# Attention with whole probabilities and one masked triangle of value differences; steps around two stage boundaries and the last norm rewritten

## The chip, the cores and the metric

The kernel runs on one core of one Trainium2 chip. The metric is the device time of one execution in microseconds (us); the time of a kernel is the median of its runs. The engines are named as in the profile: PE is TensorE (matrix products), DVE is VectorE, ACT is ScalarE, POOL is GpSimd, and SP is SyncE, which here only issues DMA transfers.

## The reference

One layer over 1024 tokens of width 2048, all in float32. What is computed:

```
h = x @ w_in + b_in                      # 2048 -> 4352 columns: q, k, v, g_attn, u_pool, g_pool
a = attention(q, k, v) * silu(g_attn)    # 16 heads of 64, 2 key/value heads, window 128, sinks, relative bias
b = pool(u_pool) * silu(g_pool)          # trailing means over 2, 4, 8, 16 tokens, minus the token, a linear map
mix = concat(a, b) @ w_out
ple = sigmoid(x @ w_gate_ple) * (p @ w_ple)
out = layer_norm(2 ** 0.25 * x + mix + ple)

# attention, for each block of 128 queries q against the block before (old) and its own block (cur):
e = exp(scores - m);  probs = e / (sum(e) + exp(sink - m))
out = probs @ [v_old; v_cur]
```

In a block, query `qq` sees the keys of the block before at positions above `qq`, and those of its own block at positions up to `qq`. So the two halves of a row of probabilities fill complementary triangles of one 128 by 128 matrix.

## The kernel before, in words

**Products.** Every large product (`x @ w_in`, `x @ w_gate_ple`, `mix @ w_out`) is done by a Strassen-Winograd scheme: seven products `p1` to `p7` in place of eight, on operand sums named `b11`, `b21`, `b22`, `t1` to `t4` (the activations' side) and on sums of weight quarters. A float32 operand is split into a high part and a rest in the fp32r format (`wh` and `wl` for weights, `b11h` and `b11l` and so on for activations), and one product is three fp32r matmuls, `wh*xh`, `wh*xl`, `wl*xh` (`mm3`, L180 to L185), over four slices of 128: twelve matmuls. The casts to the high part run on ACT (`copy`, L802 to L808, shown as L805), the rests on DVE (`lo`, L131, shown as L126 like all of DVE's two-input operations). Weight splits are made four products ahead (`take`, L245; the pool `w` has four buffers).

**Jobs and groups.** A `Job` is a pair of 128-row output blocks, and a group is one job or two side by side (`run_group`, L439). After each product the program's own clock `tick()` (L162) moves one step. `after(n, fn)` puts a step n ticks on; `later(n, fn)` does the same and makes the step's instructions stand behind the latest marked instruction of each engine (L167). A scheduler orders each engine's queue under these constraints; each queue then runs in order. Results are copied from the PSUM banks `qa`, `qb`, `sc` into tiles named `part` or `d`: by ACT for the first contribution (L421), by DVE for the second (`gather`, L416). When a job is through, `finished` (L429) adds the other half from DRAM by an accumulating DMA on POOL's queue (L434, `part<-h`), and `job.wait` ticks later `job.done` uses the tile.

**Stages** (L1123 to L1139, run from L1235 on): s1 and s2 make q, k, v and the first halves of the rest; while s2 runs, the 16 calls of `heads` (L562) do attention between the products, nine ticks apart (L1267). s3 makes second halves, with gates, pooling and the embedding gate in `done`. Its last four jobs are the attention gates: `gate_attn` (L683) applies SiLU on ACT (L685), multiplies on DVE and stores to `cc`. During its last two groups `set_by_twos` (L392) loads the operands of the next stage in pairs of tiles `two` and splits them (ACT casts, DVE rests). s4 and s5 are the output product for the two halves of its inner dimension, s5 over the first 768 tokens; s6 does the last 256 tokens with plain products (`run_plain`, L497). The last two jobs of s5 add straight onto loaded tiles (`filled`, `add_to`).

**Attention.** `heads` works on two heads for 512 queries. Per block of 128 queries: `score` (L585, scores on PE, bias and row maximum on DVE), `softmax` (L606, exponentials on ACT; L617 adds the old half onto the current half on POOL, which is lawful because the triangles don't overlap), `share` (L619, division by the sum). Per pair of blocks `trans` (L625) transposes on PE, casts the high part on ACT (L632), takes the rest on DVE (L633), and on POOL cuts each of the two into two triangles (L639): four selections of 128 by 512. `value` (L643) then multiplies the four triangles of a block with the values of the block before and of its own: four matmuls. Work tiles `s` come from the pool `slots` (16 buffers).

**Norm.** The squares are summed over blocks in s5 and s6; `norm_scale` (L1010) forms one over the standard deviation per token as a column (POOL's power, L1019), makes it a diagonal matrix (ACT L1024, or for the last 256 tokens DVE L1027) and multiplies by a matrix of ones, so that each partition holds the row of scales (L1007 and L1033). `norm_out` and `norm_out_two` apply it and store the output.

## Time and profile before

| what | value |
|---|---|
| time, median of 3 runs (lowest to highest) | 1461.7 us (1460.07 to 1462.81) |
| the profiled execution: its own time, and its span | 1460.25 us, 1458.5 us |
| VectorE, ScalarE and GpSimd busy, share of the span | 1120.4 us (77%), 788.9 us (54%), 292.6 us (20%) |
| mean granted clock of TensorE | 0.996 |
| DMA | 307.67 MB, mean 211 GB/s |

A span runs from the first to the last instruction; 1.75 us of the profiled execution's time lie around it. A row of the time line gives the start, the length, the engine, the line, the operation and its tiles, and in brackets how long the engine stood idle before it and what ended that. Matmuls overlap, so that the distance from one start to the next tells more than a length. A row of stretches gives busy microseconds of PE, of weight loads, DVE, ACT and POOL with counts, then the granted clock, the busy share of the DMA engines and GB/s.

### The profile page before, as it was taken

The page shows a single profiled execution, that of the slowest core. Times are in us where ns is not written, and L with a number is a line of the kernel's source. Part 1 is how long each engine was busy: PE and PEld are TensorE (multiplying, and loading weights), DVE is VectorE, ACT ScalarE, POOL GpSimd, SP SyncE. Part 2 cuts the span into 40 slices and gives each one's busy share as a digit, 9 for nine tenths or more (in the row PEclk, how much of TensorE's full clock was granted, in tenths as well). Part 3 has the DMA queues.
Part 4 walks back from the last instruction along what each step waited for, and adds up shares of the span by engine and source line. Part 5 has one row for each costly group of instructions (what it writes and reads, how often), then busy time and mean ns, then how long its engine had stood idle before and what let it go on. Part 6 is the DMA issues. An engine that isn't in the chain of part 4 may idle for free.

```text
span 1458.5 us, 20547 instructions
## 1 busy us (share of the span) xinstructions
PE 1435.3 (98%) x6930; PEld 1216.8 (83%) x6930; DVE 1120.4 (77%) x2031; ACT 788.9 (54%) x1560; POOL 292.6 (20%) x412
## 2 busy tenths in 40 slices
PE   9999999999999999999999999999998999999996
PEld 7888888888888888888888888888887888899996
DVE  6859578888787887888777876866777566977786
ACT  6546376565665666566655444333456333554475
POOL 1000203333233332223011111211001111111233
PEclk9999999999999999999999999999999999999998
DMA  9463885554456555557787779998698778595465
GB/s 356 181 242 117 235 222 180 172 176 152 138 181 209 182 170 176 183 194 234 200 248 221 200 216 317 318 290 247 191 347 255 190 189 232 133 268 114 120 240 207
DMA packets 112297, 307.67 MB, mean 211 GB/s; under 512 B 12800, under 2 KB 18304, under 8 KB 112192
## 3 DMA queue, kind: packets, MB, share of 16 engines
q1 hardware_dynamic: 87552, 225.88, 45.1%
q0 software_dynamic: 21312, 73.15, 21.2%
q10 hardware_dynamic: 3328, 7.34, 1.5%
q8 instruction: 54, 0.88, 0.3%
q14 instruction: 51, 0.42, 0.1%
HBM read 207.75 MB, written 98.57 MB: 210 GB/s over the span
## 4 chain that ended last, share of the span: by engine, by line
PE 64%; issue 22%; DVE 5%; POOL 4%; ACT 3%; DMA 2%; POOLq 0%; SPq 0%; ACTq 0%; DVEq 0%
PE qa L183 11%; PE qa L185 11%; PE qa L184 11%; PE qb L183 8%; PE qb L184 8%; PE qb L185 8%; POOL part L434 2%; PE sc L594 1%; PE pv L652 1%; DVE s L126 1%; DVE wl L126 1%; PE tr L630 1%; DMA part<-h 1%; DVE part L126 1%; PE sc L183 1%
## 5 line engine op out<-in xcount | busy, mean ns | idle before, releaser
L805 ACT CAST wh<-raw 128x512 fp32r<-128x512 f32 x428 | 264.0, 619 | 395.8 <-PE qa L184 143.5
L126 DVE TENSOR_TENSOR wl<-raw,wh 128x512 fp32r<-128x512 f32 x428 | 300.1, 705 | 108.6 <-ACT wh L805 105.5
L421 ACT COPY part<-qa 128x512 f32<-128x512 f32 (+1 forms) x180 | 103.9, 577 | 78.6 <-PE qa L185 76.2
L639 POOL TENSOR_SCALAR_AFFINE_SELECT s<-s 128x512 fp32r<-128x512 f32 x128 | 102.5, 813 | 132.2 <-ACT s L632 97.0
L126 DVE TENSOR_TENSOR part<-part,qb 128x512 f32<-128x512 f32 (+1 forms) x120 | 81.1, 676 | 46.4 <-PE qb L185 39.3
L183 PE MATMUL qa<-b11h,wh 128*128 128x512 f32 (+2 forms) x292 | 109.4, 375 | 0.8 <-ACT wh L805 0.8
L183 PE MATMUL qb<-b21h,wh 128*128 128x512 f32 (+2 forms) x292 | 109.2, 374 | 0.0
L185 PE MATMUL qa<-b11h,wl 128*128 128x512 f32 (+2 forms) x292 | 108.8, 373 | 0.0
L184 PE MATMUL qa<-b11l,wh 128*128 128x512 f32 (+2 forms) x292 | 108.7, 372 | 0.0
L185 PE MATMUL qb<-b21h,wl 128*128 128x512 f32 (+2 forms) x292 | 108.6, 372 | 0.0
L184 PE MATMUL qb<-b21l,wh 128*128 128x512 f32 (+2 forms) x292 | 108.6, 372 | 0.0
L183 PE MATMUL qb<-t1h,wh 128*128 128x512 f32 (+1 forms) x260 | 101.3, 390 | 3.5 <-ACT wh L805 2.0
L183 PE MATMUL qa<-t3h,wh 128*128 128x512 f32 (+1 forms) x260 | 100.6, 387 | 2.0 <-ACT part L421 2.0
L183 PE MATMUL qa<-t2h,wh 128*128 128x512 f32 (+1 forms) x260 | 100.8, 388 | 1.1 <-ACT part L421 0.5
L185 PE MATMUL qa<-t2h,wl 128*128 128x512 f32 (+1 forms) x260 | 99.9, 384 | 0.7 <-DVE wl L126 0.7
L183 PE MATMUL qb<-b22h,wh 128*128 128x512 f32 (+1 forms) x260 | 100.4, 386 | 0.0
L184 PE MATMUL qb<-t1l,wh 128*128 128x512 f32 (+1 forms) x260 | 100.3, 386 | 0.0
L185 PE MATMUL qb<-t1h,wl 128*128 128x512 f32 (+1 forms) x260 | 100.2, 386 | 0.0
L183 PE MATMUL qa<-t4h,wh 128*128 128x512 f32 (+1 forms) x260 | 100.1, 385 | 0.0
L184 PE MATMUL qa<-t3l,wh 128*128 128x512 f32 (+1 forms) x260 | 99.7, 384 | 0.0
L185 PE MATMUL qb<-b22h,wl 128*128 128x512 f32 (+1 forms) x260 | 99.7, 383 | 0.0
L184 PE MATMUL qb<-b22l,wh 128*128 128x512 f32 (+1 forms) x260 | 99.7, 383 | 0.0
(330 smaller groups left out, 3567.1 us busy)
## 6 DMA issues: line engine op xcount, KB each, us to landing
raw<-in_win SPq DMA_DIRECT2D x65, 512.0 KB, 4.1
h<-part SPq DMA_DIRECT2D x34, 512.0 KB, 2.9
part<-h POOLq DMA_DIRECT2D x34, 512.0 KB, 6.5
cw<-in_wout SPq DMA_DIRECT2D x64, 256.0 KB, 3.2
raw<-in_wgate SPq DMA_DIRECT2D x32, 512.0 KB, 4.8
raw<-wc SPq DMA_DIRECT2D x32, 512.0 KB, 4.5
s<-in_x SPq DMA_DIRECT2D x44, 256.0 KB, 6.3
wc<-cw SPq DMA_DIRECT2D x32, 256.0 KB, 2.4
```

The lines of the kernel that those rows point to most:

```text
L126: return (eng or self.nc.vector).tensor_tensor(out=out, in0=a, in1=b, op=op)
L183: mm(ps, wh, xh, start=start, stop=False, skip_group_check=True)
L184: mm(ps, wh, xl, start=False, stop=False, skip_group_check=True)
L185: return mm(ps, wl, xh, start=False, stop=stop, skip_group_check=True)
L421: self.mark("ACT", self.nc.scalar.copy(out=dst, in_=ps))
L434: self.nc.gpsimd.dma_start(out=t, in_=job.first(job.b[i]), accum_op=ALU.add)
L594: nc.tensor.matmul(ps[:, e, z:], q, kk[:, keys], start=i == 0, stop=i == 1)
L630: nc.tensor.transpose(ps[:, o : o + P], sc[bq + i][:, e, P:], self.ident)
L639: nc.gpsimd.affine_select(out=o4, in_=a4, pattern=[[0, 4], [sign, P]], compare_op=ALU.is_ge, fill=0.0, base=0 if side else -1, channel_mul ...
L652: nc.tensor.matmul(ps[:, bq % 2], self.vv[b // 4][:, b % 4], pt[bq // 2, s, i][:, o : o + 256], start=(s, i) == ms[0], stop=(s, i) == ms[-1])
L805: ins = self.nc.scalar.copy(out=out, in_=a)
```

## The change

**Attention.** `trans` keeps the transposed probabilities whole: per block it casts the high part and the rest (two casts and two rests of 128 by 256 where there was one of each of 128 by 512), and POOL cuts one triangle, the old one, of both parts at once: one selection of 128 by 512 per block, none for the first block of the sequence. `value` multiplies the whole with the values of the own block, and the old triangle with the differences (values of the block before minus own values), so that the sum is the same. `v_build` makes these differences (`vd`, new tiles `d0`, `d1`) by copies on ACT and subtractions on DVE. Their room is taken from the work tiles: 15 of 512 columns while attention runs, then 16 of 528 again in s3.

**End of s3.** Three more `part` buffers (8 where there were 5), 4 buffers for operand pairs (6 before), 8 work tiles (10 before); pairs are loaded two units ahead of their split instead of three, the first at ticks 5 and 7 (0, 3 and 6 before). The last two jobs wait 5 and 6 ticks (3 and 3 before) for `done`, their second blocks one tick more.

**s5 and s6.** Weight casts of the `filled` and plain jobs are marked, so that steps put off by `later` stand behind them on ACT. The plain operand of s6 (`last_operand`) is split at ticks 6, 8, 10 and 12 of the last group of s5 by `later`, instead of in code behind it. `norm_scale` makes no diagonal matrix: PE takes the column itself, read 128 times, as the stationary matrix, and the identity as the moving one, 128 columns at a time.

**Start.** One weight half of the embedding is loaded and split ahead of the second half of `p`, and the second and third early product change places.

The diff, cut to its core (the line numbers of the order's rows for the changed kernel are its own):

```
     def __init__(self, w, b0, b1, half, first, done, tokens=2 * T, plain=False, ahead=None):
-        self.ahead, self.filled, self.mean, self.wait = ahead, False, False, 4
+        self.ahead, self.filled, self.mean, self.apart, self.wait = ahead, False, False, False, 4
...
-        self.unit_latest = [self.copy(hi, src).ins, L.lo(lo, src, hi).ins]
+        cast = self.copy(hi, src)
+        if job.filled or job.plain:
+            self.mark("ACT", cast)
+        self.unit_latest = [cast.ins, L.lo(lo, src, hi).ins]
...
             self.split_unit(u, r.pop(u))
-            fetch(i + 3)
+            fetch(i + 2)
...
-            fetch(0)
-            self.after(3, lambda: fetch(1))
-            self.after(6, lambda: fetch(2))
+            self.after(5, lambda: fetch(0))
+            self.after(7, lambda: fetch(1))
...
-        self.later(job.wait, lambda: job.done(job.b[i], t))
+        self.later(job.wait + (i if job.apart else 0), lambda: job.done(job.b[i], t))
...
-            nc.scalar.copy(out=v[:, :, 0:64], in_=ps[:, :, g])
-            self.lo(v[:, :, 64:128], ps[:, :, g], v[:, :, 0:64])
+            d = self.vd[h] = self.tile(self.kv, [P, 3 + h, P], f"d{h}", F32R)
+            at = slice(1 - h, 4)
+            s = self.slot()
+            v32, d32 = (s[:, i * 256 : i * 256 + 256].rearrange("p (b d) -> p b d", b=4) for i in range(2))
+            nc.scalar.copy(out=v32, in_=ps[:, :, g])
+            nc.scalar.copy(out=v[:, :, 0:64], in_=v32)
+            self.lo(v[:, :, 64:128], v32, v[:, :, 0:64])
+            if h:
+                self.tt(d32[:, 0], self.vv[0][:, 3, 0:64].bitcast(F32), v32[:, 0], ALU.subtract)
+                self.tt(d32[:, 0], d32[:, 0], self.vv[0][:, 3, 64:128].bitcast(F32), ALU.add)
+            self.tt(d32[:, 1:4], v32[:, 0:3], v32[:, 1:4], ALU.subtract)
+            nc.scalar.copy(out=d[:, :, 0:64], in_=d32[:, at])
+            self.lo(d[:, :, 64:128], d32[:, at], d[:, :, 0:64])
...
-            hi, lo = self.slot(), self.slot()
-            nc.scalar.copy(out=hi.bitcast(F32R)[:, :T], in_=ps)
-            self.tt(lo.bitcast(F32R)[:, :T], ps, hi[:, :T], ALU.subtract)
-            for i, a in enumerate((hi, lo)):
-                for side, o in enumerate((self.slot(F32R), a)):
...
+            for i in range(2):
+                t = ps[:, 2 * i * P : 2 * i * P + 2 * P].rearrange("p (e q) -> p e q", e=2)
+                both = pt[bq + i] = self.slot(F32R)[:, :T].rearrange("p (s e q) -> p s e q", s=2, e=2)
+                nc.scalar.copy(out=both[:, 0], in_=t)
+                self.lo(both[:, 1], t, both[:, 0])
+                if not k0(bq + i):
+                    a = old[bq + i] = self.slot(F32R)[:, :T]
+                    nc.gpsimd.affine_select(out=a.rearrange("p (c q) -> p c q", c=4), in_=both.rearrange("p s e q -> p (s e) q").bitcast(F32), pattern=[[0, 4], [-1, P]],
+                                            compare_op=ALU.is_ge, fill=0.0, base=-1, channel_multiplier=1)
...
+            ms = [(self.vv[h][:, bq], pt[bq].rearrange("p s e q -> p (s e q)"))]
+            if not k0(bq):
+                ms.append((self.vd[h][:, bq - 1 + h], old[bq]))
...
-        self.load(first[:, 1], w[:, 1])
+            if not h:
+                self.load(first[:, 1], w[:, 1])
...
-        dg = L["new"]("dg")
...
+        each = [rstd[:, b : b + 1].broadcast_to([P, P]) for b in range(n)]
...
+                        nc.tensor.matmul(ps[:, b * P - i : b * P - i + P], each[b], self.ident, start=b * P == i, stop=True, skip_group_check=True)
...
-            j.wait = 3 if j in s3[-2:] else 5 if j in s3[-4:-2] else 4
+            j.wait = 5 if j in s3[-4:-1] else 6 if j is s3[-1] else 4
...
+        for j in s3[-2:]:
+            j.apart = True
...
-            self.ple_half(0, 1, (("qa", 2), ("qa", 2)))
+            self.ple_half(1, 0, (("qa", 2), ("qa", 2)))
...
-        self.slots = self.work_pool("slots", 16, work)
+        self.slot_n = T
+        self.slots = self.work_pool("slots0", 15, work)
...
-                self.slots = self.work_pool("slots1", 10, work)
-                self.twos = self.work_pool("twos1", 6, work)
+                six[:] = 5 * [pp] + 3 * [self.work_pool("p8", 3, work)]
+                self.slots = self.work_pool("slots1", 8, work)
+                self.twos = self.work_pool("twos1", 4, work)
+                self.new_part = part_of_six
...
+            if i == n5 - 1:
+                for k in range(4):
+                    self.later(6 + 2 * k, lambda k=k: last_operand(k))
             self.run_group(g + i)
```

How the queues stand, at three places. First ACT's queue in the last group of s3, at the products that `part<-qb` copies out: `two` are the operand pairs, `t1h` the next stage's third operand, and the words in brackets are the semaphores waited for (DMAHW and DMASW are transfers). Before:

```order
L421 COPY part_10632<-qb_10737 128x512 [waits DMAHW6_49,PE_49]
L805 CAST wh_10781<-raw_10532 128x512 [waits DMAHW7_49,DVE_49,PE_49]
L805 CAST t1h_10838<-two_10608 128x1024 [waits DMAHW1_49,PE_49]
L421 COPY part_10634<-qb_10757 128x512 [waits DMAHW0_49,DVE_49,Activation_49]
L805 CAST t1h_10838<-two_10610 128x1024 [waits DMAHW2_49]
```

Now:

```order
L423 COPY part_10647<-qb_10752 128x512 [waits DMAHW4_49,PE_49]
L815 CAST wh_10796<-raw_10547 128x512 [waits DMAHW5_49,DVE_49,PE_49]
L423 COPY part_10649<-qb_10772 128x512 [waits PE_49]
L815 CAST t1h_10849<-two_10720 128x1024 [waits DMAHW5_49]
L815 CAST t1h_10849<-two_10722 128x1024 [waits DMAHW6_49]
```

The second copy no longer waits for a transfer, and it stands ahead of the two casts. Second, ACT's queue where s3 ends and s4 begins: L685 (now L695) is the SiLU of the last attention gates, `wh` the weights of s4's first products. Before:

```order
L805 CAST wh_11006<-s_2189_11001 128x512 [waits DVE_49,PE_49,Activation_49]
L421 COPY part_10965<-qa_10973 128x512 [waits DMAHW1_49,PE_49]
L685 ACTIVATE part_10631<-part_10631,cst 128x1024 [waits DMASW0_49]
L685 ACTIVATE part_10632<-part_10632,cst 128x1024 [waits DMASW2_49,Activation_49]
L805 CAST wh_11037<-s_2193_11032 128x512 [waits DVE_49,PE_49]
L805 CAST wh_11055<-raw_10556 128x512 [waits PE_49]
L421 COPY part_10967<-qa_11010 128x512 [waits DMASW4_49,Activation_49]
```

Now:

```order
L815 CAST wh_11017<-s_2189_11012 128x512 [waits DVE_49,PE_49,Activation_49]
L423 COPY part_10976<-qa_10984 128x512 [waits PE_49]
L423 COPY part_10978<-qa_11021 128x512 [waits PE_49]
L695 ACTIVATE part_10646<-part_10646,cst 128x1024 [waits DMASW0_49]
L815 CAST wh_11040<-s_2193_11035 128x512 [waits DVE_49,Activation_49]
L695 ACTIVATE part_10647<-part_10647,cst 128x1024 [waits DMASW2_49,Activation_49]
L815 CAST wh_11062<-raw_10567 128x512 [waits PE_49,Activation_49]
```

The copies lost their waits for transfers, and the next weight cast stands ahead of the second SiLU, not behind it. Third, DVE's queue early in the last group of s5: `d<-d,qb` adds a product and frees its bank, `b11l` is the rest of s6's plain operand, `raw` and `s` are sums of weights. Before:

```order
L126 TENSOR_TENSOR s_2549_13155<-raw_13030 128x512 [waits DMAHW3_49]
L126 TENSOR_TENSOR b11l_13400<-two_12862,b11h_13398 128x512 [waits Activation_49]
L126 TENSOR_TENSOR raw_13030<-raw_12902,raw_13030 128x512 [waits DVE_49]
L126 TENSOR_TENSOR wl_13161<-s_2549_13155,wh_13160 128x512 [waits Activation_49]
L126 TENSOR_TENSOR raw_12902<-s_2549_13155,raw_12902 128x512 [waits DVE_49]
L126 TENSOR_TENSOR d_12215<-d_12215,qb_13164 128x384 [waits PE_49]
```

Now:

```order
L126 TENSOR_TENSOR s_2549_13175<-raw_13050 128x512 [waits DMAHW3_49]
L126 TENSOR_TENSOR raw_13050<-raw_12922,raw_13050 128x512 [waits DVE_49]
L126 TENSOR_TENSOR d_12235<-d_12235,qb_13184 128x384 [waits PE_49]
L126 TENSOR_TENSOR raw_12922<-s_2549_13175,raw_12922 128x512 [waits DVE_49]
L126 TENSOR_TENSOR wl_13181<-s_2549_13175,wh_13180 128x512 [waits Activation_49]
```

`b11l`, one `wl` and one sum `raw` stood ahead of `d<-d,qb` and now stand behind it, `b11l` ten places further on.

More of the change, by code (lines that the diff above doesn't have):

```diff
@@ L837, in ple_begin @@
                 self.lo(lo, p[h][:, k], hi)
-        self.ple_split(1)
+            if not h:
+                self.ple_split(1)
     def ple_split(self, n):
@@ L858, in ple_half @@
             out = self.copy(self.ple_out[(2 * n + b) % 4][:, h], ps[b])
-        if not n:
+        if n < 2:
             self.turn["ACT"] = out.ins
@@ L1019, in norm_scale, with spread @@
         self.tt(rstd, var, self.mhalf[:, :n], ALU.pow, nc.gpsimd)
-        dg = L["new"]("dg")
-        if wait:
-            for b in range(n):
-                f = slice(b * P, b * P + P)
-                nc.scalar.activation(dg[:, f], self.ident, AF.Copy, scale=rstd[:, b : b + 1])
-        else:
-            each = [t.broadcast_to([P, n, P]) for t in (self.ident.rearrange("p (b t) -> p b t", b=1), rstd.rearrange("p (b t) -> p b t", t=1))]
-            self.tt(dg[:, : n * P].rearrange("p (b t) -> p b t", b=n), *each, ALU.mult)
+        each = [rstd[:, b : b + 1].broadcast_to([P, P]) for b in range(n)]
         if wait:
             L["a"] = L["parts"][0]
-            self.later(wait, lambda: self.norm_spread(L, L["a"], self.ones, dg))
+            def spread():
+                for i, e in L["cut"]:
+                    ps = self.bank("sc", 2)[:, : e - i]
+                    for b in range(i // P, e // P):
+                        nc.tensor.matmul(ps[:, b * P - i : b * P - i + P], each[b], self.ident, start=b * P == i, stop=True, skip_group_check=True)
+                    nc.scalar.copy(out=L["a"][:, i:e], in_=ps)
+            self.later(wait, spread)
         else:
             L["a"] = self.bank("sc", 2)[:, : L["n"]]
-            nc.tensor.matmul(L["a"], self.ones, dg[:, : L["n"]], start=True, stop=True)
+            for b in range(n):
+                nc.tensor.matmul(L["a"][:, b * P : b * P + P], each[b], self.ident, start=b == 0, stop=True, skip_group_check=True)
     def norm_out(self, L, j):
@@ L1210, in first @@
             self.split_part("b11", 1, a[:, 1])
[L1211 removed]
+            self.ple_half(0, 1, (("qb", 2), ("qb", 2)))
             self.split_part("b11", 2, b)
@@ L1284, in run @@
                 over.close()
-                over = ExitStack()
+                work.close()
+                work, over = ExitStack(), ExitStack()
+                self.slot_n = T + 16
+                self.slots = self.work_pool("slots", 16, work)
                 self.extras = self.work_pool("e2", 6, over)
@@ L1314, in run @@
         csum = []
-        p6 = []
-        def part_of(b):
-            pool = pp
-            if p6:
-                p6.append(p6.pop(0))
-                pool = p6[-1]
-            return self.tile(pool, [P, 2, T], "part")
-        self.new_part = part_of
         def co_done(b, c):
@@ L1347, in run @@
                 work = ExitStack()
+                at = next(i for i, p in enumerate(six) if p is not pp)
+                six[:] = [p for p in six if p is pp]
+                six.insert(at, self.work_pool("p6", 1, work))
                 self.twos = self.work_pool("twos2", 8, work)
-                p6.extend(5 * [pp] + [self.work_pool("p6", 1, work)])
                 d0 = self.work_pool("d0", 4, work)
```

46 lines of the change are left out of this document (19 added, 27 removed).

## The prediction

> **What bounds the kernel now.** I read the page first, for the share of each engine.
>
> ```profile
> span 1458.5 us, 20547 instructions
> PE 1435.3 (98%) x6930; PEld 1216.8 (83%) x6930; DVE 1120.4 (77%) x2031; ACT 788.9 (54%) x1560; POOL 292.6 (20%) x412
> ```
>
> PE is busy for 1435.3 of 1458.5 us. The change leaves its large products alone, and a block of attention still takes four value matmuls. So no more than the idle 23.2 us can be won, and the question is which of them the edits reach. The busy time by stretch tells where they lie (first figure: length; second: PE busy).
>
> ```profile
> 0.00:40.00 40.00, 38.03 (x162) 31.18 (x163) 28.86 (x40) 24.35 (x38) 3.68 (x13) 1.00 0.87 337
> 400.00:500.00 100.00, 98.15 (x493) 82.15 (x492) 83.78 (x195) 63.76 (x159) 34.80 (x43) 1.00 0.53 185
> 1000.00:1100.00 100.00, 98.22 (x433) 80.82 (x432) 70.94 (x107) 48.42 (x73) 6.98 (x8) 1.00 0.86 266
> 1100.00:1200.00 100.00, 98.05 (x426) 80.62 (x425) 65.35 (x93) 41.70 (x65) 16.89 (x24) 0.98 0.76 207
> 1300.00:1400.00 100.00, 98.61 (x582) 97.11 (x581) 74.61 (x119) 48.62 (x84) 18.00 (x26) 1.00 0.55 142
> 1400.00:1458.50 58.50, 45.63 (x365) 43.47 (x363) 44.67 (x80) 41.76 (x72) 20.68 (x38) 0.93 0.63 220
> ```
>
> Idle are 1.97, 1.85, 1.78, 1.95, 1.39 and 12.87 us. The last is mostly the end, where the norm is applied and stored behind the last matmul. I then asked each stretch who ended PE's idle time, and followed the releaser's own queue on the time line.
>
> **End of s3, first stall: -1.8 us.** PE, ACT and SP:
>
> ```profile
> 1095.93 0.50 PE L183 MATMUL qa<-t3h,wh 128*128 128x512 f32 x1 [1.78 <-ACT part L421]
> 1093.34 0.59 ACT L421 COPY part<-qb 128x512 f32<-128x512 f32 x1 [2.34 <-DMA cc<-part]
> 1085.54 2.31 SPq L140 DMA_DIRECT2D cc<-part  x2
> ```
>
> ACT stands 2.34 us at a copy into a `part` buffer that is still being stored to `cc`, and PE runs out of free banks behind it. With eight buffers the copy waits for PE alone (the first pair of orders), so this goes: 1.78 us. What is late next are the casts `t1h`, whose pairs are now loaded one unit later; that is a rival below.
>
> **End of s3, second stall: -3.6 us.**
>
> ```profile
> 1121.56 1.15 ACT L685 ACTIVATE part<-part,cst 128x1024 f32<-128x1024 f32 x1 [4.14 <-DMA part<-h]
> 1111.16 0.89 POOL L434 DMA_DIRECT2D part<-h  x1 [2.05 <-ACT part L421]
> 1125.39 0.69 PE L183 MATMUL qb<-t1h,wh 128*128 128x512 f32 x1 [1.95 <-ACT wh L805]
> 1125.40:1128.80 3.40, 3.40 (x8) 2.70 (x9) 3.40 (x7) 3.40 (x5) 0.00 (x0) 0.51 0.39 157
> ```
>
> The second SiLU waits 4.14 us for an accumulating transfer issued at 1111.16, and the weight cast behind it comes 1.95 us late for PE. This `done` now comes three ticks later (from 3 to 5 + 1). A tick is one product of twelve matmuls, and the stretch from 1000 to 1100 us has 433 of them in 98.22 us, 0.227 each: 2.7 us a tick, 8.2 us for three, more than the 4.14 us missed. The second pair of orders shows the weight cast ahead of that SiLU as well. The loads of `pre` move with it by two ticks; the stores to `cc` go by POOL's queue, whose next accumulating transfers come fourteen products on, when s4's first group is through, and `cc` is read a stage later. The `part` buffers stay taken longer, four by s3 and four by s4: exactly the eight that there are. Behind the stall the last row shows 3.40 us at a granted clock of 0.51, hence another 3.40 x 0.49 = 1.7 us. Together 1.95 + 1.7 = 3.65.
>
> The row shows half the clock behind an idle time of 1.95 us. The Trainium skill, "TensorE: Matmul & The Clock Gate", section "Part 1: The HAM clock gate", has the clock fall only after an idle window of about 3.4 us; by that rule this pause would cost no clock, the term would be 1.95 and the sum 1.7 us smaller. The row decides, though the pause may meet the clock's window otherwise in another execution: -2.0 is the near end of this term.
>
> **Last group of s5: -1.2 us.**
>
> ```profile
> 1369.95 0.44 PE L183 MATMUL qa<-t2h,wh 128*128 128x384 f32 x1 [0.40 <-ACT wh L805]
> 1371.38 0.44 PE L183 MATMUL qb<-t1h,wh 128*128 128x384 f32 x1 [0.82 <-DVE d L126]
> 1367.73 1.13 ACT L1399 CAST b11h<-two 128x512 fp32r<-128x512 f32 x2
> 1368.37 0.69 DVE L126 TENSOR_TENSOR b11l<-two,b11h 128x512 fp32r<-128x512 f32 x1
> 1370.79 0.54 DVE L126 TENSOR_TENSOR d<-d,qb 128x384 f32<-128x384 f32 x1
> ```
>
> The plain operand's casts and rest slipped in ahead of the weight cast and of the addition PE waited for. They now come ticks later, and the third pair of orders puts three operations of some 0.6 us behind the addition: more than 0.82. The last of them is due at tick 12 of 14; at 98.61 / 582 = 0.17 us a matmul (the stretch from 1300) two ticks are 4 us, and cast and rest take 1.3: s6 finds its operand ready. The mark adds a wait: squares and later `norm_out` stand behind a weight cast on ACT; DVE's sums wait for these squares, and nobody waits for the sums until the group is over. At nothing, with that cover.
>
> **s6: -0.4 us.** While the first 768 tokens are normed:
>
> ```profile
> 1405.50:1435.50 30.00, 28.79 (x236) 27.79 (x235) 29.88 (x52) 28.29 (x43) 15.28 (x28) 1.00 0.92 328
> 1400.26 1.87 ACT L1024 ACTIVATE q<-ident,st 128x128 f32<-128x128 f32 x6 [2.44 <-POOL st L126]
> ```
>
> DVE is busy for 29.88 of 30 us: it bounds here, and PE loses 1.21. DVE's order stays as it was, so marking ACT's casts does not help. The diagonal matrices free 1.87 us of ACT and a wait of 2.44 in front, so that DVE can have about one rest `wl` (0.69, row below) done before the rush. That is a third to a half of the loss; I take a third, and the ends are 0 and -1.2.
>
> **The norm's columns: -0.4 us.**
>
> ```profile
> 1446.61 0.72 POOL L126 TENSOR_TENSOR st<-st,mhalf 128x2 f32<-128x2 f32 x1 [13.23 <-DVE st L1018]
> 1447.37 0.43 DVE L126 TENSOR_TENSOR t2l<-ident,st 128x256 f32<-128x256 f32 x1 [0.84 <-POOL st L126]
> 1447.85 0.70 PE L1033 MATMUL sc<-t2l,ones 128*128 128x256 f32 x2 [1.51 <-DVE t2l L126]
> 1402.58 1.45 PE L1007 MATMUL sc<-q,ones 128*128 128x512 f32 x4
> ```
>
> At the end everything hangs on this chain, and DVE's 0.43 us go. PE moves the same columns, 256 here and 768 at 1402.58, in pieces of 128 with more weight loads. No row shows a stationary matrix read from one column; if it loads like any other, PE's part stays at 0.70 and 1.45. Ends: -0.5 and, were the two pieces to take twice the 0.70, +0.3.
>
> **Attention: -0.9 us.** PE's waits from 150 to 700 us, and the rows that price the edit (groups: busy, mean ns):
>
> ```profile
> PE qa L183 <- ACT part L421: 0.7, 3, 0.3
> PE qb L183 <- DVE part L126: 0.7, 1, 0.7
> PE qa L185 <- DVE wl L126: 0.7, 1, 0.7
> PE sc L594 <- DVE s L126: 0.6, 2, 0.4
> L639 POOL TENSOR_SCALAR_AFFINE_SELECT s<-s 128x512 fp32r<-128x512 f32 x128 | 102.5, 813 | 132.2 <-ACT s L632 97.0
> L632 ACT CAST s<-tr 128x512 fp32r<-128x512 f32 x32 | 18.7, 586 | 11.1 <-PE tr L630 11.0
> L126 DVE TENSOR_TENSOR s<-tr,s 128x512 fp32r<-128x512 f32 x32 | 21.8, 683 | 1.9 <-ACT s L632 1.8
> L551 ACT CAST v<-tr 128x256 fp32r<-128x256 f32 x3 | 1.1, 374 | 0.5 <-PE tr L549 0.5
> L126 DVE TENSOR_TENSOR v<-tr,v 128x256 fp32r<-128x256 f32 x3 | 1.3, 424 | 0.2
> 404.27 2.12 POOL L639 TENSOR_SCALAR_AFFINE_SELECT s<-s 128x512 fp32r<-128x512 f32 x2
> 404.79 1.12 DVE L126 TENSOR_TENSOR wl<-raw,wh 128x512 fp32r<-128x512 f32 x1
> 410.01 0.69 DVE L126 TENSOR_TENSOR wl<-raw,wh 128x512 fp32r<-128x512 f32 x1 [0.98 <-ACT wh L805]
> ```
>
> Selections: 128 (four for each of 32 pairs of blocks) become 56 (one for each of 64 blocks, less the sequence's first in each of 8 pairs of heads), so POOL loses 72 x 0.813 = 58 us. ACT: 64 x 0.374 - 32 x 0.586 = +5.2 us; DVE: 64 x 0.424 - 32 x 0.683 = +5.3; the value differences add some twenty pieces of at most 0.4. Against this DVE's same operation takes 1.12 us under a selection and 0.69 without: 0.43 per selection, so 0 to 72 x 0.43 = 31 us return to DVE. All is off PE's path but for the 2.7 us of the first four rows, of which 0.7 waits for the very `wl` that selections slow. I take a third off; ends -2.7 and, with one work tile fewer, +3.
>
> **Start: 0.** PE's early wait is for the second quarter of `p`, whose place in the queue does not change:
>
> ```profile
> 6.57 0.62 ACT L836 CAST t4h<-two 128x512 fp32r<-128x512 f32 x1 [1.82 <-DMA two<-in_p]
> ```
>
> **Sum.** -1.8 - 3.6 - 1.2 - 0.4 - 0.4 - 0.9 = -8.3 us. On the profiled execution's 1460.25 that is 1452.0; the median of the runs shown, 1461.7, lies 1.45 above it and would give 1453.4. I forecast 1452.5.
>
> **The rivals.**
>
> *Late pairs (0.14).* Operand pairs come one unit later into a full DMA system:
>
> ```profile
> two<-pt SPq DMA_DIRECT2D x8, 512.0 KB, 7.9
> ```
>
> A pair issued once DVE frees its buffers has about two units, 16 us, to its split; SP's later weight loads queue behind a pair that waits for a buffer. 7.9 us fits. If landings double, ACT stands at `t1h` as it stood at `cc`: 1.8 us return with 1.7 of slow clock, and the time is 1452.5 + 3.5 = 1456.
>
> *Attention gets slower (0.07).* One work tile fewer and two more pieces per pair of blocks push ACT and DVE into PE's path. The point from which this decides: the other terms give -7.4, so it takes over 0.46 us for each of 16 head calls; at one more cast and one more rest (0.374 + 0.424 = 0.8) it is 12.8 - 7.4 = +5.4, 1467. Against it: DVE is 84% and ACT 64% busy in the 400 to 500 row. For it: the Trainium skill, "VectorE: DVE Perf Modes", section "Rules for kernel authors", advises to keep the number of operations down, and this edit raises it.
>
> *The stalls only move (0.09).* What PE gains at one place it loses at the next wait of ACT: 1460 to 1461.
>
> *All of it goes (0.10).* The waits of attention and of s6 vanish too: 2.7 and 1.2 instead of 0.9 and 0.4, 1449.9.
>
> **How the numbers follow.** The forecast has 0.60. A measurement of this kernel can tell about 0.2%, 2.9 us, from no change. Forecast, late pairs and all of it are faster by more: 0.84; moving stalls are the same: 0.09; attention: 0.07. The range goes from 1447.2 (all of it, less the 2.7 by which the three runs before differ) to 1459.0 (late pairs, with the second stall's clock term of 1.7 and s5's 1.2 kept as well): it leaves out the slower rival and the unmoved one, 0.16 together.
>
> **What would show it.** Right: no idle time over 1 us and a clock of 1.00 from 1085 to 1130 us; no wait of PE at the start of s5's last group; DVE still full in s6; 0.4 us less between POOL's power and the first scaling; about 45 us of selections. Wrong: waits `<-DMA two<-pt` on ACT ahead of PE's; new waits on `s` between 150 and 700; a longer PE group at the norm's columns.

## The result, and the profile after

The changed kernel takes 1451.36 us (median of 4 runs, 1450.59 to 1453.36) against 1460.88 us for the kernel before (4 runs beside it, 1459.64 to 1462.81). The ratio is 0.9937, with a 95% interval of 0.9922 to 0.9952. The forecast was 1452.5. The profiled execution took 1451.2 us, with a span of 1449.5. From the page of the changed kernel:

```profile
span 1449.5 us, 20551 instructions
PE 1433.2 (99%) x6940; PEld 1216.7 (84%) x6940; DVE 1117.7 (77%) x2074; ACT 794.6 (55%) x1594; POOL 235.1 (16%) x340
```

PE's work is what it was, its idle time is 16.3 us in place of 23.2, and POOL has lost 57.5 us, as 72 selections fewer should give. The busy time by stretch, for the same stretches as before (the last row is s6, shifted by the 9 us that this kernel is ahead there):

```profile
0.00:40.00 40.00, 38.45 (x166) 31.52 (x167) 28.75 (x39) 24.39 (x38) 3.45 (x13) 1.00 0.88 337
400.00:500.00 100.00, 100.00 (x508) 84.70 (x508) 85.37 (x217) 68.09 (x179) 22.05 (x27) 1.00 0.56 195
1000.00:1100.00 100.00, 100.00 (x442) 82.64 (x441) 73.75 (x111) 49.35 (x73) 6.96 (x8) 1.00 0.85 268
1100.00:1200.00 100.00, 98.15 (x431) 80.37 (x430) 64.52 (x93) 41.65 (x66) 17.41 (x25) 1.00 0.77 207
1300.00:1400.00 100.00, 99.82 (x617) 98.96 (x616) 77.00 (x124) 51.88 (x90) 18.50 (x27) 1.00 0.52 143
1396.50:1426.50 30.00, 28.79 (x237) 27.94 (x236) 29.18 (x50) 28.36 (x43) 15.22 (x28) 1.00 0.89 313
```

Gained are 1.85 us from 400 to 500, 1.78 from 1000 to 1100 and 1.21 from 1300 to 1400. From 1100 to 1200 PE still loses 1.85, though at a clock of 1.00 where it was 0.98, and s6 loses its 1.21 as before.

To see what each part brings, I cut every trace at the same matmuls of PE's time line and took the distances between their starts: the first score (`sc<-kh`), the last value product (`pv<-s`), the last 512-wide product (end of s4), the last 384-wide one (end of s5), the last 256-wide one (end of s6), and the end of PE's last matmul. Such distances, in us, for each kernel of this study, from one profiled execution each:

| kernel | start | attention | s3 and s4 | s5 | s6 | last sums |
|---|---|---|---|---|---|---|
| before | 195.53 | 503.94 | 568.90 | 123.90 | 52.52 | 3.75 |
| changed | 195.37 | 500.32 | 565.18 | 122.35 | 52.46 | 3.81 |
| e1, attention alone | 196.05 | 503.36 | 568.38 | 124.09 | 52.56 | 3.75 |
| e2, end of s3 alone | 196.28 | 504.49 | 562.72 | 124.06 | 52.63 | 4.28 |
| e3, changed, selections twice | 195.09 | 502.48 | 564.92 | 122.20 | 52.42 | 3.30 |
| e4, changed, pairs early | 195.30 | 502.08 | 562.55 | 122.08 | 52.43 | 3.31 |
| e5, before, smaller pieces | 196.91 | 504.60 | 567.67 | 123.82 | 52.48 | 3.75 |
| e6, before, half the selections | 195.60 | 501.27 | 567.89 | 123.95 | 52.48 | 4.24 |
| e7, before, operand moved | 196.72 | 504.56 | 568.72 | 122.16 | 52.50 | 4.27 |
| e8, e4 with a wider spread | 194.96 | 500.94 | 562.73 | 122.16 | 50.13 | 3.30 |
| e9, start alone | 194.81 | 504.36 | 568.10 | 123.81 | 52.49 | 3.75 |
| e10, e8 with whole pieces | 196.74 | 503.29 | 562.42 | 122.31 | 50.10 | 3.31 |

What follows the last matmul is 9.96 to 9.98 us in all of them. Kernels that share the code of a stage show how far one execution is to be trusted: s5 and s6 repeat within 0.3 us, s3 and s4 within some 1.3 (the old end of s3), the start within about 2, and the attention within 0.6 with the old code and 3.0 with the new. "PE's loss" in the expectations below is the same reading made finer: for each matmul the distance to the next one's start, less the median distance of its kind, summed over a stretch. The sums shift with how the kinds are cut (with kinds by shape alone the stretch from 400 to 500 us has 4.0 before and 1.0 after, not 5.0 and 1.6), so only their differences are to be read.

What was left at the end of s3 in the changed kernel, on the time lines of ACT, PE and SP:

```profile
1105.21 1.05 ACT L815 CAST b22h<-two 128x1024 fp32r<-128x1024 f32 x1 [2.67 <-DMA two<-cc]
1112.05 1.05 ACT L815 CAST t4h<-two 128x1024 fp32r<-128x1024 f32 x1 [2.79 <-DMA two<-pt]
1106.80 0.50 PE L183 MATMUL qa<-b11h,wh 128*128 128x512 f32 x1 [0.57 <-ACT part L423]
1119.23 0.47 PE L183 MATMUL qb<-t1h,wh 128*128 128x512 f32 x1 [1.26 <-ACT wh L815]
1098.09 0.53 SPq L140 DMA_DIRECT2D two<-cc  x1
1098.85 1.46 SPq L140 DMA_DIRECT2D two<-pt  x2
```

Both old stalls (idle 1.78 and 1.95) are gone. Two new ones (0.57 and 1.26) stand behind casts that waited 2.67 and 2.79 us for operand pairs. The second tile of the pair for `b22h` was issued at 1098.09 and landed at 1105.19, after 7.1 us; that for `t4h` was issued at 1099.98 and landed at 1112.03, after 12. ACT was ready for them at 1102.54 and 1109.26 (start of the cast less the wait), 4.5 and 9.3 us behind the issue.

### The profile page after: what moved, and what is told of

It reads as the page before. It is cut to its first block, busy times and chain, and to the rows that moved or that the text cites. A ratio compares the mean times of both kernels' runs of the same rounds, so it can differ in the third digit from the quotient of the medians.

```text
span 1449.5 us, 20551 instructions
## 1 busy us (share of the span) xinstructions
PE 1433.2 (99%) x6940; PEld 1216.7 (84%) x6940; DVE 1117.7 (77%) x2074; ACT 794.6 (55%) x1594; POOL 235.1 (16%) x340
## 4 chain that ended last, share of the span: by engine, by line
PE 95%; DMA 1%; DVE 1%; ACT 1%; issue 1%; POOL 0%; POOLq 0%; SPq 0%; ACTq 0%; DVEq 0%
PE qa L183 16%; PE qa L185 16%; PE qa L184 16%; PE qb L183 12%; PE qb L184 12%; PE qb L185 12%; PE sc L607 2%; PE pv L663 2%; PE sc L185 1%; PE sc L183 1%; PE sc L184 1%; DMA two<-pt 1%; PE tr L643 1%; ACT wh L815 0%; DVE raw L126 0%
## 5 line engine op out<-in xcount | busy, mean ns | idle before, releaser
L126 DVE TENSOR_TENSOR wl<-raw,wh 128x512 fp32r<-128x512 f32 x428 | 296.6, 696 | 108.0 <-ACT wh L815 103.4
L185 PE MATMUL qa<-t3h,wl 128*128 128x512 f32 (+1 forms) x260 | 99.8, 384 | 0.0
L184 PE MATMUL qa<-t2l,wh 128*128 128x512 f32 (+1 forms) x260 | 99.8, 384 | 0.0
```

The lines of the kernel that those rows point to most:

```text
L126: return (eng or self.nc.vector).tensor_tensor(out=out, in0=a, in1=b, op=op)
L184: mm(ps, wh, xl, start=False, stop=False, skip_group_check=True)
L185: return mm(ps, wl, xh, start=False, stop=stop, skip_group_check=True)
```

## The experiments

The experiments ran in three sets, each on another chip, with the kernel before beside each: 1461.17 us beside e1 to e4, 1461.33 beside e5 to e8, 1462.38 beside e9 and e10. Theory A said that the gains lie at separate places and add up; the rivals are named at each run.

**e1, the attention part alone.** The kernel before with the edits of `v_build`, `trans`, `value` and the work tiles:

```
-            hi, lo = self.slot(), self.slot()
-            nc.scalar.copy(out=hi.bitcast(F32R)[:, :T], in_=ps)
...
+                both = pt[bq + i] = self.slot(F32R)[:, :T].rearrange("p (s e q) -> p s e q", s=2, e=2)
+                nc.scalar.copy(out=both[:, 0], in_=t)
+                self.lo(both[:, 1], t, both[:, 0])
```

Expected:

> The kernel before with the attention part of the change alone (whole probabilities, one triangle per block, differences of values, 15 work tiles). Theory A: the attention part is worth about what PE lost less between 150 and 700 us in the two traces, 13.0 - 8.8 = 4.2 us, so 1456.5 to 1457.5 against 1460.9 before, with PE's waits for ACT part, DVE part and DVE wl between 400 and 700 us gone and the stalls at 1094 and 1123 us still there. Rival B, the prediction's own term: 0.9 us, 1460, and the rest of the 4.2 belongs to the other parts.

Measured: 1459.33 us (12 runs), ratio 0.9981 (0.9970 to 0.9992), that is 1.2 to 4.4 us less. From 400 to 500 us PE's loss falls from 5.0 to 1.6 us as in the whole change, but from 600 to 700 it is 4.9 in place of 3.2. The stretch, and PE's two longest waits from 150 to 700 us:

```profile
400.00:500.00 100.00, 100.00 (x508) 84.68 (x508) 85.63 (x216) 67.41 (x178) 22.05 (x27) 1.00 0.55 192
PE sc L605 <- DVE s L126: 0.8, 3, 0.4
PE sc L605 <- DVE st L607: 0.4, 1, 0.4
```

The loss from 600 to 700 differs between executions of the same code (3.2 before, 3.9 in e2, 3.6 in e7), with the new code more so: PE is idle there for 0.03 us in the changed kernel, 0.45 in e8, 0.90 in e4 and 1.62 in e1. So the 4.2 us between the two traces were the edit and some luck of that execution. The stalls at 1094 and 1123 us stay, as expected; PE's waits between 400 and 500 go, those between 600 and 700 don't. The part is worth 2 to 3 us (four executions with it take 501.7 us in the mean for the attention, four with the old code 504.3, by the table), neither 4.2 nor 0.9.

**e2, the end of s3 alone.** The kernel before with eight `part` buffers, four pair buffers, eight work tiles, later pairs and later `done`:

```
-            j.wait = 3 if j in s3[-2:] else 5 if j in s3[-4:-2] else 4
+            j.wait = 5 if j in s3[-4:-1] else 6 if j is s3[-1] else 4
...
+                six[:] = 5 * [pp] + 3 * [self.work_pool("p8", 3, work)]
+                self.slots = self.work_pool("slots1", 8, work)
+                self.twos = self.work_pool("twos1", 4, work)
```

> The kernel before with the edits at the end of s3 alone (eight part buffers, four pair buffers, later pairs, later done). Theory A: the two old stalls (1.9 and 2.1 with 1.7 of slow clock) go and two new ones at late pairs (0.7 and 1.4) come, net -3.5: 1457.4 against 1460.9 before, with ACT waiting for two<-cc and two<-pt at the casts of the last pairs. Rival B: the late pairs are chance of one execution, and this part alone brings the predicted 5.4 us: 1455.5, with no idle time of PE over 0.5 us from 1085 to 1130.

Measured: 1456.26 us, ratio 0.9959 (0.9944 to 0.9974); s3 and s4 take 562.72 us, 6.2 less than before and 5.6 less than the mean of the six kernels with that stage as before (568.28). The two stretches, and ACT's longest wait for a pair:

```profile
1000.00:1100.00 100.00, 100.00 (x442) 82.62 (x441) 71.51 (x109) 49.34 (x75) 6.97 (x8) 1.00 0.85 272
1100.00:1200.00 100.00, 99.79 (x441) 82.29 (x440) 67.98 (x96) 44.07 (x69) 17.42 (x25) 1.00 0.79 216
1109.64 1.05 ACT L804 CAST b22h<-two 128x1024 fp32r<-128x1024 f32 x1 [1.90 <-DMA two<-cc]
```

Rival B came closer: of the predicted 5.4 us the stage shows 5.6 and the time 4.9 (3.8 to 8.2 by the interval), and no idle time of PE from 1085 to 1130 us is over 0.21. The pairs are late here too, but by 1.9 us, not 2.7 and 2.8, and PE loses 0.4. So 1.9 us of lateness was all but covered by the products that PE had in hand here, and 2.7 was not in the changed kernel.

**e3, each selection twice.** The changed kernel, every selection issued a second time with the same operands:

```
+                    for _ in range(2):
                         nc.gpsimd.affine_select(out=a.rearrange("p (c q) -> p c q", c=4), in_=both.rearrange("p s e q -> p (s e) q").bitcast(F32), pattern=[[0, 4], [-1, P]],
```

> The changed kernel with each selection done twice on POOL, the second writing the same again: 112 selections in place of 56, near the 128 of before. Theory A (selections slow DVE's operations with two SBUF inputs, and these make PE wait): 2 to 4 us of the attention gain return, 1453.5 to 1455.5 against 1451.4 for the changed kernel, DVE's wl under a selection near 0.8 to 1.1 us again and more of them. Rival B (the gain comes from casts and rests in smaller pieces and another order on ACT and DVE, not from POOL): within 0.5 us of the changed kernel, 1451.4.

Measured: 1452.21 us (1450.55 to 1454.05), ratio to the kernel before 0.9932 (0.9914 to 0.9951). POOL's group and the stretch:

```profile
L652 POOL TENSOR_SCALAR_AFFINE_SELECT s<-s 128x512 fp32r<-128x512 f32 x112 | 89.5, 807 | 160.4 <-DVE s L126 107.8 <-issue 18.4 <-DVE b11l L126 16.0
400.00:500.00 100.00, 100.00 (x508) 84.69 (x507) 87.26 (x216) 67.47 (x178) 31.77 (x39) 1.00 0.56 195
```

With POOL nearly as busy as before (31.77 against 34.80) PE still loses nothing from 400 to 500. DVE is slowed as theory A says (busy 87.26 against 85.37 for the same work; the `wl` that overlap POOL's work take 860 ns in the mean between 150 and 700 us, against 801 in the changed kernel), but PE does not wait for it there. The attention takes 502.48 us, within the 500.3 to 503.4 of the four other kernels with the new code and below the old ones' 503.9 to 504.6. Theory A's 2 to 4 us did not return; 0.85 did, by the medians, less than the intervals can tell.

**e4, pairs early.** The changed kernel with the old loads of pairs, paid for with one `part` buffer and two work tiles:

```
-            fetch(i + 2)
+            fetch(i + 3)
...
-            self.after(5, lambda: fetch(0))
-            self.after(7, lambda: fetch(1))
+            fetch(0)
+            self.after(3, lambda: fetch(1))
+            self.after(6, lambda: fetch(2))
...
-                six[:] = 5 * [pp] + 3 * [self.work_pool("p8", 3, work)]
-                self.slots = self.work_pool("slots1", 8, work)
-                self.twos = self.work_pool("twos1", 4, work)
+                six[:] = 5 * [pp] + 2 * [self.work_pool("p8", 2, work)]
+                self.slots = self.work_pool("slots1", 6, work)
+                self.twos = self.work_pool("twos1", 6, work)
```

> The changed kernel with the pairs loaded three units ahead again, as before (at ticks 0, 3 and 6, six pair buffers), with seven part buffers in place of eight and six work tiles in place of eight to make the room. Theory A (the late pairs cost the two stalls of 0.7 and 1.4 us at 1106 and 1118): both go, 1449.3 against 1451.4, and ACT's waits for two<-cc and two<-pt are under 0.5 us. Rival B (the DMA system is full there, so that earlier pairs only push other transfers later): the waits move to weights, part<-h or s<-pre, and the time is 1451.4 or above.

Measured: 1449.27 us, ratio 0.9913 (0.9897 to 0.9930); the stage takes 562.55 us.

```profile
1000.00:1100.00 100.00, 100.00 (x442) 82.62 (x441) 74.62 (x112) 48.77 (x74) 6.98 (x8) 1.00 0.86 269
1100.00:1200.00 100.00, 100.00 (x443) 82.81 (x442) 66.34 (x95) 41.67 (x67) 17.45 (x25) 1.00 0.76 212
```

Theory A holds to a tenth: both late-pair stalls go and ACT waits for no pair from 1085 to 1130 us. Rival B's full DMA system (busy 0.86) carries the earlier pairs without delaying anything that PE needs.

**e5 and e6, the attention part taken apart.** Two edits of the kernel before. e5 does the cast and the rest of a pair of blocks in two halves and keeps the four selections; e6 leaves out the selections of the own triangle and keeps the whole casts:

```
+            for f in (slice(0, T // 2), slice(T // 2, T)):
+                nc.scalar.copy(out=hi.bitcast(F32R)[:, f], in_=ps[:, f])
+                self.tt(lo.bitcast(F32R)[:, f], ps[:, f], hi[:, f], ALU.subtract)
...
+                    if side == 0:
                         nc.gpsimd.affine_select(out=o4, in_=a4, pattern=[[0, 4], [sign, P]], compare_op=ALU.is_ge, fill=0.0,
```

> The kernel before with one thing of the attention part: the cast and the rest of each pair of blocks done in two pieces of 128x256 instead of one of 128x512; the four selections stay. The signal is PE's loss from 400 to 500 us (start to start over the median), 5.0 us before, 1.6 with the attention part. Theory B (smaller pieces let a weight's cast and rest through sooner): it falls to about 1.6 us and the time by about 3, to 1458. Theory A (the number of selections counts): it stays near 5.0, and the time at 1461 or up to 2 us above it, by the added operations.

> The kernel before with the selections of the own triangle left out (64 of 128 stay; the value product then takes unmasked rows for the own block, so the output is another); casts and rests are as before. Theory A (the number of selections counts): PE's loss from 400 to 500 us falls from 5.0 to about 1.6, the time to about 1458, and fewer wl stand under a selection. Theory B (the smaller pieces and their order count): the loss stays near 5.0 and the time within 1 us of 1461.

Measured: e5 1461.50 us, ratio 1.0005 (0.9996 to 1.0013); e6 1457.12 us, ratio 0.9969 (0.9959 to 0.9979). The stretch from 400 to 500 us in e5, and in e6 with POOL's group and PE's longest wait between 150 and 700 us:

```profile
400.00:500.00 100.00, 99.12 (x498) 82.89 (x497) 83.18 (x208) 64.23 (x166) 32.81 (x43) 1.00 0.54 185
```

```profile
400.00:500.00 100.00, 98.87 (x501) 83.34 (x500) 83.38 (x198) 64.69 (x163) 21.54 (x29) 1.00 0.55 190
L640 POOL TENSOR_SCALAR_AFFINE_SELECT s<-s 128x512 fp32r<-128x512 f32 x64 | 49.2, 769 | 137.4 <-ACT s L632 100.1 <-DVE b11l L126 15.3 <-DVE s L126 9.0
PE qa L185 <- DVE wl L126: 0.6, 1, 0.6
```

By the times smaller pieces alone bring nothing, and half of the selections alone brings 3.1 to 6.0 us, with 2.7 to 3.3 us less in the attention than the four executions of the old code. PE's loss from 400 to 500 is 4.0 in e5 and 3.0 in e6: neither reaches the 1.6 of the whole edit, so that this one stretch is not decided by either alone. Its idle time there says the same, and repeats well: 1.54 to 1.85 us in four executions of the old code, 0.88 in e5, 1.13 in e6, and none in five of the new code. Theory A is right that leaving selections out gains, but the number alone does not explain it, since e3 put 56 back at little cost. One reading fits both and was not tested: e6 and the changed kernel leave out the selections of the own triangle, which stood between the rest and the own block's value product, while e3 doubles those of the old triangle alone.

**e7, the operand alone.** The kernel before with `last_operand` put off by `later` and the marked casts:

```
+        if job.filled or job.plain:
+            self.mark("ACT", cast)
...
+            if i == n5 - 1:
+                for k in range(4):
+                    self.later(6 + 2 * k, lambda k=k: last_operand(k))
```

> The kernel before with only the plain operand of s6 split by later steps inside the last group of s5, and weight casts marked for it. From the end of the 512-wide products to the last 384-wide one it took 123.9 us before and 122.1 to 122.4 in three kernels with the whole change. Theory A (the operand's casts ahead of the weight's cast and of the addition are the cause): 122.4 here, the stalls of 0.6 and 1.0 us at 1369 and 1370 gone, the time about 1459.5. Rival B (the norm without diagonal matrices brings it, by freeing ACT): 123.9, and the stalls stay.

Measured: 1460.45 us, ratio 0.9993 (0.9984 to 1.0003), too small for the times to tell from none; s5 took 122.16 us against 123.8 to 124.1 in six kernels without the edit.

```profile
1300.00:1400.00 100.00, 99.82 (x592) 98.96 (x591) 76.34 (x121) 49.44 (x85) 18.95 (x27) 1.00 0.58 148
```

PE is busy for 99.82 as in the whole change, where it was 98.61. Both stalls are gone, so this edit is the whole gain of s5 and the norm's new columns have no part in it.

**e8, a wider spread.** e4 with the norm of the first 768 tokens spread further over s6:

```
-            self.later(7 + 17 * j // 16, lambda j=j: self.norm_out(one, j))
+            self.later(7 + 22 * j // 16, lambda j=j: self.norm_out(one, j))
```

> The kernel with early pairs (seven part buffers, six pair buffers, six work tiles) and the norm of the first 768 tokens spread over 22 ticks of s6 in place of 17. Theory A (DVE bounds s6 while the norm's multiplications crowd it): the three stalls of 0.56 us shrink, from the last 384-wide to the last 256-wide product 51.2 us or less in place of 52.4, and 1448.1 in place of 1449.3. Rival B (DVE's weight rests set the pace by themselves): 52.4 as it was, and the end later, if the last tokens' stores then wait.

Measured: 1445.81 us (1445.42 to 1447.03), ratio 0.9895 (0.9881 to 0.9908): it beats both kernels, by 15.5 us that of before. s6 takes 50.13 us in place of 52.43. The same 30 us of s6:

```profile
1394.00:1424.00 30.00, 30.00 (x257) 30.00 (x256) 29.11 (x52) 27.47 (x44) 14.14 (x26) 1.00 0.83 287
```

PE loses nothing and does 257 matmuls in place of 237; DVE is as full as it was. What happened there in the changed kernel is seen at one of its three stalls, on PE and ACT:

```profile
1418.30 0.39 PE L183 MATMUL qa<-b11h,wh 128*128 128x256 f32 x1 [0.41 <-ACT wh L815]
1415.62 1.03 ACT L129 ACTIVATE part<-part,cst 128x768 f32<-128x768 f32 x1 [0.26 <-DVE part L126]
1417.63 0.62 ACT L815 CAST wh<-raw 128x512 fp32r<-128x512 f32 x1 [0.15 <-ACT t2l L1003]
```

PE waits for a weight's cast, which comes on ACT behind the norm's scaling (1.03 us), which waited 0.26 us for DVE's multiplication. Both queues are nearly full there (DVE 29.18 and ACT 28.36 of 30 us), and which of them sets the pace is not told by these rows. That the norm's steps crowd the weights' casts is shown by e8: with fewer of them in a tick, all fit.

**e9, the start alone.** The kernel before with the new order of the first loads and products:

```
-            self.ple_half(0, 1, (("qa", 2), ("qa", 2)))
+            self.ple_half(1, 0, (("qa", 2), ("qa", 2)))
...
-            self.ple_half(1, 0, (("qb", 2), ("qb", 2)))
+            self.ple_half(0, 1, (("qb", 2), ("qb", 2)))
```

> The kernel before with the edits of the start alone (one weight half of the embedding ahead of the second half of p, second and third early product changed over). Up to the first score product six executions with the start of before took 195.5 to 196.9 us (mean 196.2), four with the new start 195.0 to 195.4 (mean 195.2). Theory A (the order of the first loads and products is worth 1 us): 195.2 here and a time of about 1460.3 against 1461.3. Rival B (it is the landing of p, which varies from one execution to the next): 196.2 and 1461.3.

Measured: 1460.72 us, ratio 0.9992 (0.9982 to 1.0002); 194.81 us to the first score. That speaks for theory A, but e10, with the same start, took 196.74. The means are 196.2 for six old starts and 195.4 for six new ones; both lie within what one start varies by. This stays open.

**e10, whole pieces.** e8 with one cast and one rest per pair of blocks and two selections, the value products with differences kept:

```
+            hi, lo = pt[bq // 2] = [self.slot(F32R)[:, :T] for _ in range(2)]
+            nc.scalar.copy(out=hi, in_=ps)
+            self.lo(lo, ps, hi)
+            old[bq // 2] = [self.slot(F32R)[:, :T] for _ in range(2)]
```

> The kernel with early pairs and the norm spread over 22 ticks, with one cast and one rest of 128x512 for each pair of blocks as before the change, and two selections of 128x512 for the pair (64 in all, where it had 56 and two casts and two rests); the value products with differences stay. Theory A (fewer selections are the gain of the attention part, and the smaller pieces give some of it back): ACT and DVE lose some 5 us of busy time each between 150 and 700 us, from the first score to the last value product 500.5 us or less (500.9 with pieces), and 1445.0 to 1445.8 against 1445.8. Rival B (the pieces help): 502 us or more there, and 1447 or above.

Measured: 1447.79 us (1445.76 to 1450.72), ratio 0.9906 (0.9891 to 0.9921), 2 us above e8 by the medians; the attention takes 503.29 us against 500.94. The stretch and PE's longest wait:

```profile
400.00:500.00 100.00, 98.53 (x498) 82.90 (x498) 86.09 (x206) 64.79 (x162) 23.68 (x29) 1.00 0.52 182
PE qa L185 <- DVE wl L126: 1.0, 1, 1.0
```

From 150 to 700 us ACT and DVE lose 6.7 and 7.1 us of busy time, as expected, and PE loses more. Theory A's second half (the pieces cost) is not borne out. The times do not tell e10 from e8: the intervals of the ratios overlap, and e1, with pieces, took 503.36 in the attention too. The stretch from 400 to 500 does, as far as one execution goes: PE is idle there for 1.47 us, and for none in the five executions with pieces and differences, e3 with its 112 selections among them. So rival B holds in this stretch: together with the differences, the smaller pieces help.

## Why the prediction was right, point by point

The forecast was -8.3 us and the profiled execution has -9.05. The end of s3, s5 and the norm's columns went by the predicted mechanism; s6 did not, the attention was under-sized, and a rival, the late pairs, took place beside the forecast. That the sum came within a microsecond is partly luck: the late pairs cost some 2.5 us that the sum did not have, and the attention brought some 1.8 to 2.7 more than it had. "Measured" is the difference of the stage from the kernel before in the table above, where nothing else is said.

| term | predicted | measured |
|---|---|---|
| end of s3, both stalls | -1.8 - 3.6 | -5.6 alone (e2, from the mean of six kernels); -3.7 in the changed kernel, with late pairs (-3.1 from that mean) |
| last group of s5 | -1.2 | -1.55; -1.7 alone (e7) |
| s6 | -0.4 | -0.06 |
| the norm's columns | -0.4 | +0.06; -0.45 at equal clock |
| attention | -0.9 | -3.6 in one execution, -2.7 in the mean of four |
| start | 0 | -0.2 in one execution; open |

**End of s3, first and second stall.** Both went as argued, and alone (e2) the part brings the predicted amount. But the term of 1.7 for the slow clock was the price of one execution. Of six with the old end of s3, three show it (before, e5, e9); in the others (e1, e6, e7) the clock stays at 1.00 and PE stalls a third time instead, for 1.35 to 1.37 us, behind DVE's `part`. Before, then e7 with PE's third wait from 1085 to 1140 us:

```profile
1085.00:1135.00 50.00, 46.27 (x196) 37.44 (x195) 39.31 (x54) 31.18 (x44) 5.89 (x9) 0.97 0.86 276
1085.00:1135.00 50.00, 44.55 (x194) 35.94 (x194) 40.10 (x55) 30.27 (x42) 5.88 (x9) 1.00 0.87 285
PE qb L183 <- DVE part L126: 1.4, 1, 1.4
```

The stage takes as long either way (568.2 us in the mean of the three with the half clock, 568.3 without), so the sum of the term is right, while the clock need not be what is paid.

The rival "late pairs" then took place as well, at `two<-pt`, which the prediction named as a sign, and at `two<-cc`. Its price was 2.5 us (565.18 against 562.7 in e2, e4 and e8), not 3.5: the stalls left the clock at 1.00. The argument against it, that a landing of 7.9 us fits into 16, failed first on the 16: the tiles were issued 4.5 and 9.3 us before ACT was ready for them. The one for `b22h` landed within 7.1 us and was late all the same; the one for `t4h` took 12, where 7.9 would have fitted. The sign that the prediction asked for, no idle over 1 us, was missed by the 1.26 us at 1119.23.

**Last group of s5.** Right in its place and cause. The size was read from the brackets (0.40 and 0.82), while the distances from start to start were longer than the median by 0.56 and 0.98. A bracket runs from the modelled end of the matmul before, 0.33 us after its start, while these 384-wide matmuls follow one another at 0.17 (0.39 and 0.227 for the 512-wide ones); so it understates a stall by 0.16. The first and second stall of s3 were 1.94 and 2.11 by this reading, in place of 1.78 and 1.95.

**s6.** The near end of the term, 0. Two steps failed. The first is "it bounds here", said of DVE for its busy time. In the kernel before, as in the changed one, PE's three stalls wait for ACT's casts:

```profile
PE qa L183 <- ACT wh L805: 0.8, 2, 0.4
PE qb L183 <- ACT wh L805: 0.4, 1, 0.4
```

DVE's busy time fell from 29.88 to 29.18 of 30 us and PE gained nothing; in e8 DVE is busy for 29.11 and PE loses nothing. The second is the head start (one rest of 0.69 us would also be over half of the loss of 1.21, not a third to a half). The weights' rests did come earlier at the beginning of the rush, 4.6 us ahead of PE's first use against 1.8 to 3.2 before (end of a rest to the start of its first matmul, on the two time lines). But this lead fell to 2.2 us within two products and then by some 0.35 with each, and was gone before the rush was over.

**The norm's columns.** The term is right and was hidden in this execution. At the end of the changed kernel, then of e4, where the same matmuls ran at full clock (rows of the time line and of the stretch):

```profile
1438.28 1.22 PE L1047 MATMUL sc<-ident,st 128*128 128x128 f32 x4 [1.05 <-POOL st L126]
1438.20:1439.50 1.30, 1.22 (x4) 0.93 (x4) 0.00 (x0) 0.00 (x0) 0.03 (x1) 0.50 0.00 0
```

```profile
1437.03 0.71 PE L1048 MATMUL sc<-ident,st 128*128 128x128 f32 x4 [1.06 <-POOL st L126]
1436.80:1437.80 1.00, 0.71 (x4) 0.52 (x4) 0.02 (x1) 0.00 (x0) 0.18 (x1) 1.00 0.00 0
```

At a clock of 1.00 the last sums take 3.30 us with columns (e3, e4, e8, e10) and 3.75 with the diagonal matrix (before, e1, e5, e9): -0.45, DVE's 0.43 as argued. The longer PE group, a sign of being wrong by the prediction, did show (1.22 us), but by the clock and not by the columns. A stationary matrix read from one column costs PE what a dense one does, 0.71 against 0.70. Which execution has the half clock there is not in the edit's hands, as the old form had it too, in e2:

```profile
1443.20:1444.50 1.30, 1.22 (x2) 0.50 (x2) 0.00 (x0) 0.00 (x0) 0.00 (x0) 0.50 0.00 0
```

**Attention.** The term was under-sized: 2.7 by the means of e1's paragraph. "I take a third off" the 2.7 us of four rows; but the rows list only waits, and PE also lost time in smaller steps: 13.0 us over the medians from 150 to 700, 8.8 after. Leaving out the selections of the own triangle is a cause (e6); whether it is their number or their place ahead of the value product stays open (e3). How much the smaller pieces add depends on what stands beside them (nothing by the time of e5; in e10 1.5 us of PE's idle time from 400 to 500), and by which step of the order is not settled: the busy times of DVE and ACT do not tell it, since in e10 they fall while PE's idle time rises. The rival "attention gets slower" did not occur: DVE has 1.6 and ACT 4.3 us more to do from 400 to 500 than before, and both fit. Nor was e5, with more operations alone, any slower (ratio 1.0005).

**Start.** ACT's second cast began at 5.65 us in place of 6.57:

```profile
5.65 0.62 ACT L847 CAST t4h<-two 128x512 fp32r<-128x512 f32 x1 [0.84 <-DMA two<-in_p]
```

The piece of `p` that it waits for landed at 5.63, but at 5.54 in e1 with the old order too, so this row is the transfer's own variation, as the term of 0 had it.

## What to carry to other kernels

Price a stall by the distance from start to start, less what is usual there, not by the idle time in brackets; and where one buffer is given to one queue, ask how long before its use each transfer of the other queue can still be issued, and what it will take when the DMA system is at its fullest, not in the median. A busy engine is not yet the bound: before calling it one, look which single instruction the next engine waits for, and what stands ahead of it in that queue. A gain below the spread of single executions is found by cutting the traces at the same instructions, over several kernels that share the stage.

## What was not expected of the hardware

The granted clock of TensorE fell to 0.50 behind an idle time of 1.05 us (the changed kernel at 1438.28) and stayed at 1.00 behind idle times of 1.26 us in the same execution (1119.23) and of 1.06 in e4, and even of 2.51 (e7 at 1127.00). So an idle time of a given length does not decide it here. The Trainium skill, "TensorE: Matmul & The Clock Gate", section "Part 1: The HAM clock gate", asks for an idle window of about 3.4 us; no pause of that length precedes the row at 1438.28.

Where the time falls seems to matter. The half clock at the second stall lasts 3.413 us in each of the three executions that have it (before, e5, e9). Each begins 324.27 us, some 95.0 times 3.413, ahead of the fall at the end of the same trace, though the matmul that ends the stall starts anywhere from 0.54 us before to 0.34 us after it. Counted in such steps back from the last fall, PE was busy for 0.43, 0.33 and 0.34 of the 3.413 us ahead of these three falls, and for 0.62, 0.50 and 0.52 of the like stretch at the second stall of e1, e6 and e7, where the clock stayed. This fits a clock that is decided anew every 3.413 us by how busy PE has just been. It is not the whole rule: ahead of the row at 1438.28 the share is 0.66, with matmuls of a single column among them.

DVE's operations with two inputs in SBUF are slowed while POOL works, and those with one input in PSUM are not: in the trace of before, from 150 to 700 us, `wl` takes 839 ns in the mean of 50 that overlap POOL's work for 0.2 us or more and 688 in the mean of 82 that don't, while `part<-part,qb` takes 680 and 682.
